# Two-layer PEER decoder trunk: zero columns of the activations written by ScalarE instead of VectorE, small transfers for 16 gathered tokens begun by GpSimd, an index conversion placed later, and one pacing constant 2.0 → 1.85

## The chip, the cores and the metric

The kernel runs on one core of a Trainium2 chip. The metric is the device time of one execution in microseconds (us). Five engines work side by side, each taking its own instructions in order: TensorE (PE, matmul; its weight loads are listed as PEld), VectorE (DVE), ScalarE (ACT), GpSimd (POOL) and SyncE (SP), which here only starts transfers (DMA). An engine's instruction can wait for another engine's or a transfer's semaphore, and what stands behind it on the same engine then waits too.

## The reference, cut

512 tokens of 1024 features pass two layers. Each layer has a mixer (pooling and retention in layer 0, a gated linear recurrence in layer 1) and then PEER, a product-key expert layer, which is where the change lies:

```python
def block(xt):                                   # tokens x 1024
    q = (xt @ w_q).reshape(T, 8, 2, 128)
    s = jnp.einsum('thpd,hpkd->thpk', q, sub_keys)
    s_top, i_top = lax.top_k(s, 16)
    cand = s_top[:, :, 0, :, None] + s_top[:, :, 1, None, :]     # 16 x 16 sums
    cand_id = i_top[:, :, 0, :, None] * 128 + i_top[:, :, 1, None, :]
    best, pos = lax.top_k(cand.reshape(T, 8, 256), 16)
    eid = take_along_axis(cand_id, pos)          # of 16384 experts, 16 per head
    gate = softmax(best)
    act = gelu(einsum('td,thkd->thk', xt, u_tab[eid]))
    return einsum('thk,thkd->td', gate * act, v_tab[eid])
```

Then `h = layer_norm(alpha * h + peer(h))`.

## The kernel before, in words

**Two ways for two kinds of tokens.** For 368 of the 512 tokens (`TN` = 368) PEER is computed densely: all 16384 experts stand in 128 blocks of 128, and each block costs 24 matmuls against `peer_ut` (first product, `mm1`, lines L699 to L708), a gelu on ACT into a tile `ge`, a multiplication by the gate (zero for experts that a token didn't choose, DVE, L1014), and matmuls against `peer_v` (second product, L1049). f32 products are made of three products of a high and a low part: ACT makes the high part `hi` (L132) and DVE the low part `lo` (L133) of every streamed block. The last 144 tokens are not computed densely: POOL gathers their experts' rows (L926). Of these, 16 tokens (`TX`) have columns of their own in the dense accumulators, which is why `ge` has `TD` = 384 columns: the last 16 of each block are zeroed by a DVE memset (L713 in `lookahead`, L991 in `experts`; one memset for a group of `NB` = 4 blocks).

**Stages of one layer's PEER** (`peer`, L654). (1) `route_topk`: queries, top-k and softmax, nearly all on DVE; at its end the ids and gates of a tile of tokens are transposed on PE (L797) and copied into `kT` (ACT L799 to L802, DVE L803). The gates of the first 128 tokens (`gz`) are scattered by POOL with 128 small indirect transfers per layer (L90). (2) `route_gates`, for the other 240 dense tokens: for each group of 8 tokens DVE builds one-hot tiles `oh` (L856) and weighted ones `og` (L857) and PE multiplies them (L866, L867). Two groups are a pair: 32 small matmuls, 15 pairs per layer. ACT copies the result into `gbuf` (L868), and `gd<-gbuf` (2 MB, L875) writes it to memory. (3) `experts`, L954: gates are loaded (`gt<-gd` by SP, L993; `gt<-gz`, L101, the first two by POOL, later ones by SP), multiplied into `ge`, split into `ch` (ACT) and `cl` (DVE), and used by the second product, with the row gathers of POOL and their DVE work (L937, L951) beside.

**What sets the order.** While stages 1 and 2 run, the first products of 56 of the 128 blocks are made ahead of time (`lookahead`, L710) to keep PE busy. A counter (L685 to L691) adds up a cost that the routing yields and takes one block for each 2.8; in the gate stage each pair yields `2 * Y2`. Blocks not taken by the end of stage 2 follow it. `ge` has three buffers; finished groups are written to memory (`sp<-ge`, 768 KB, L719), so a group's first write to `ge` waits until the transfer of the group three before it has landed. The order of the instructions on each engine is fixed when the program is built.

**The 16 gathered tokens' table** `xg` (ids and gates) is filled from `eg` by eight transfers of 2 KB on SP's queue (L873), one per pair; DVE converts the ids to integers (`eidx`, L1001).

Of the kernel before, what the change touches and what calls it, by code (L numbers as in the profile page):

```python
# [20 lines left out]
P = 128  # L21
# [8 lines left out]
NB = 4  # L30
NG = NE // NB
TD = 3 * P
TX = 16
TN = TD - TX
GX = P // TX
GQ = 8
NSD = TD // 32
NLA = 14
# [2 lines left out]
ROT = 3  # L41
RAW = 5
QS = 8
Y2 = 2.0
YC = (0.0, 0.0, 1.0, 4.0)
AHEAD = 4
TAIL = 4
# [58 lines left out]
class Kern:  # L106
# [589 lines left out]
                tb, hs[tb], g1, b1, None if layer else xT, out if layer else None))  # L696
        return xT

    def mm1(self, layer, blk, xT, dst, alt=False):  # L699
        nc = self.nc  # L700
        uh, ul = self.stream(self.io["peer_ut"][layer, blk])
        if alt:
            ps = self.psC.tile([P, 512], F32, name="pC", tag="pC")
        else:
            ps = self.psA.tile([P, 512], F32, name="pA", tag="pA")
        self.mm3(ps[:, :TN], [((uh[:, dc * P:(dc + 1) * P], ul[:, dc * P:(dc + 1) * P]),
                               (xT[0][:, dc, :TN], xT[1][:, dc, :TN])) for dc in range(NDC)])
        nc.scalar.activation(dst[:, :TN], ps[:, :TN], AF.Gelu)  # L708

    def lookahead(self, layer, xT, sp):  # L710
        for g in range(NLA):
            ge = self.pe.tile([P, NB, TD], F32, name="ge", tag="ge", bufs=3)
            self.nc.vector.memset(ge[:, :, TN:], 0.0)  # L713
            for b in range(NB):
                self.mm1(layer, g * NB + b, xT, ge[:, b, :], b % 2 == 1)
                if g >= NLA - KEEP:
                    self.kept[g] = ge
                elif b == NB - 1:
                    self.nc.sync.dma_start(out=sp[g], in_=ge)  # L719
                yield  # L720

    def route_topk(self, layer, xT, kT, gz):
        nc, tc, io = self.nc, self.tc, self.io
        with tc.tile_pool(name="rt", bufs=1) as rt, tc.tile_pool(name="rt2", bufs=2) as rt2, \
# [14 lines left out]
            def choose(tb, h0, n):  # L739
# [47 lines left out]
                n = P - TX if tb == 2 else P  # L787
                if tb == 2:
                    eg = self.eg
                    nc.vector.tensor_copy(eg[:, :, 0], ef.rearrange("p (h s) -> p h s", h=8))  # L790
                    nc.scalar.copy(eg[:, :, 1], gate)
                tg = slice((tb - 1) * P // GW, ((tb - 1) * P + n) // GW)
                ghT, glT = kT[:, tg, 2, :], kT[:, tg, 3, :]
                yield 2.8
# [40 lines left out]
    def route_gates(self, layer, kT, iot, gd):  # L835
        nc, tc = self.nc, self.tc
        W, L = GW, 2
        Q = W // L
        with tc.tile_pool(name="rg", bufs=2) as rg:
            b5 = [P, 2, Q, P, L]  # L840
            for s in range(NSD - NSZ):
                gbuf = rg.tile([P, P, 32], F32, name="gbuf", tag="gbuf")
                if s * 32 + 32 > TN - P:
                    nc.vector.memset(gbuf[:, :, 32 - TX:], 0.0)
                for q in range(32 // W):
                    t0 = s * 32 + q * W
                    if t0 >= TN - P:
                        continue

                    def per(i):  # L850
                        v = kT[:, t0 // W, i:i + 2, :].rearrange("p i (q l) -> p i q l", l=L)
                        return v[:, :, :, None, :].broadcast_to(b5)

                    oh = rg.tile([P, 2, Q, P, L], F16, name="oh", tag="oh")
                    og = rg.tile([P, 2, Q, P, L], F16, name="og", tag="og")
                    nc.vector.tensor_tensor(oh, iot[:, None, None].broadcast_to(b5), per(0), ALU.is_equal)  # L856
                    nc.vector.tensor_tensor(og, oh[:, 1:2].broadcast_to(b5), per(2), ALU.mult)  # L857
                    for r in range(W // 4):
                        if q % 2 and r == W // 4 - 1:
                            pg = self.psC.tile([P, 512], F32, name="pC", tag="pC")  # L860
                        else:
                            pg = self.psB.tile([P, 512], F32, name="pB", tag="pB")
                        for i in range(4):
                            a, b = divmod(r * 4 + i, L)
                            sl = slice(i * P, (i + 1) * P)
                            nc.tensor.matmul(pg[:, sl], oh[:, 0, a, :, b], og[:, 0, a, :, b], start=True, stop=False)  # L866
                            nc.tensor.matmul(pg[:, sl], oh[:, 0, a, :, b], og[:, 1, a, :, b], start=False, stop=True)  # L867
                        nc.scalar.mul(gbuf[:, :, q * W + r * 4:q * W + r * 4 + 4],  # L868
                                      pg.rearrange("p (t k) -> p k t", t=4), 1.0 / GS)
                    if q % 2:  # L870
                        h = t0 // (2 * W)
                        if h < GX:
                            nc.sync.dma_start(out=self.xg[h * TX:(h + 1) * TX], in_=self.eg[P - TX:, h])  # L873
                        yield 2 * Y2
                nc.sync.dma_start(out=gd[:, :, s].rearrange("g p b t -> p g b t"),  # L875
                                  in_=gbuf.rearrange("p (g b) t -> p g b t", b=NB))
# [77 lines left out]
    def experts(self, layer, xT, hs, gd, gz, sp, norm):  # L954
        nc, tc, io = self.nc, self.tc, self.io
        with tc.tile_pool(name="ex", bufs=2) as ex, tc.tile_pool(name="ga", bufs=2) as ga:
# [10 lines left out]
            ges = {}  # L967
# [11 lines left out]
            def front(i):  # L979
                if i >= NE:  # L980
                    return
                g, b = order[i // NB], i % NB
                if b == 0:
                    if g in kept:
                        ge = self.kept[g]
                    else:
                        ge = self.pe.tile([P, NB, TD], F32, name="ge", tag="ge", bufs=3)
                    if g < NLA and g not in kept:
                        nc.sync.dma_start(out=ge, in_=sp[g])
                    elif g >= NLA:  # L990
                        nc.vector.memset(ge[:, :, TN:], 0.0)  # L991
                    gt = ex.tile([P, NSD, NB, 32], F32, name="gt", tag="gt")
                    nc.sync.dma_start(out=gt[:, NSZ:], in_=gd[g])  # L993
                    gz.read(nc.gpsimd if i < 2 * NB else nc.sync, gt[:, :NSZ], g)
                    ges[g] = (ge, gt)
                if g >= NLA:
                    self.mm1(layer, g * NB + b, xT, ges[g][0][:, b, :])

            for i in range(AHEAD):
                front(i)  # L1000
            nc.vector.tensor_copy(self.eidx, self.xg[:, 0])  # L1001
            cs, vs = [], []
            for i in range(NE):
                if i % 2 == 0:
# [2 lines left out]
                if 2 * NB <= i < 2 * NB + GX:  # L1007
                    h = i - 2 * NB
                    nc.sync.dma_start(out=xx[h * TX:(h + 1) * TX], in_=hs[2][P - TX:])
                g, b = order[i // NB], i % NB  # L1010
# [10 lines left out]
                if i < NE - TAIL and i % 2:  # L1021
                    for k in (i - 1, i):
                        for tb in range(3):
                            self.mm2(accs[tb], tb, cs[k], vs[k], k == 0, False)
                used += 1.0 if g < NLA else 2.0
                while done < (P + TX + GQ) * used / (total * 1.02):
                    done += 1
# [155 lines left out]
```

## Time and profile before

| what | value |
|---|---|
| median of 3 runs | 2825.73 us (2825.2 to 2831.99) |
| profiled execution | 2827.84 us, of it span 2826.0 us (first to last instruction) |
| mean granted PE clock | 0.995 of full |
| busy: PE, DVE, ACT, POOL | 99%, 84%, 40%, 45% |

The span is what the trace shows; 1.84 us of the profiled execution lie outside it. The two layers' gate stages run from about 418 to 524 us and from about 1878 to 1983 us of the span, the expert stages from about 553 to 1340 us and from about 2011 to 2780 us. "Granted clock" is the share of full speed (2.4 GHz) at which PE was allowed to run; 0.5 is its lower level, 1.2 GHz.

### The profile page before, as it was taken

To read this page: it belongs to the slowest core of one execution; us is meant where nothing else is said; L and a number is where in the kernel's file an instruction comes from. 1 tells how busy PE (TensorE), PEld (TensorE's weight loads), DVE (VectorE), ACT (ScalarE), POOL (GpSimd) and SP (SyncE) were. 2 spreads that over 40 slices of the span, in tenths; PEclk is the share of its full clock that TensorE was granted. 3 is DMA by queue.
4 is the path that set the end of the run, shared out by engine and by line. 5 is a ranking of instruction groups with operands and counts; after the bars stand their busy time and mean duration, and the time that the engine had idled before them with its cause. 6 is when DMAs were issued, how large, how long until landed. Compare 5 with 4: busy or idle time off the path is not lost. (4 is left out here: it accounts for less than half of the span.)

```text
span 2826.0 us, 42314 instructions
## 1 busy us (share of the span) xinstructions
PE 2786.0 (99%) x15258; PEld 2493.2 (88%) x15258; DVE 2380.9 (84%) x4802; ACT 1120.5 (40%) x1661; POOL 1276.3 (45%) x865
## 2 busy tenths in 40 slices
PE   9999989999999999999999999989999999999998
PEld 7898989988888888888788898989888988888887
DVE  6679988689888889887798689988689898889897
ACT  3334555433333333333334344555333333333332
POOL 0008777245555545543000037885345454445451
PEclk9999999999999999999999999999999999999999
DMA  6355579999999999998322545579999999999994
GB/s 227 124 187 113 138 187 264 295 354 406 356 372 365 370 380 362 355 376 287 101 82 72 204 125 120 150 198 272 339 373 377 364 373 362 379 354 374 351 372 157
DMA packets 316755, 778.32 MB, mean 275 GB/s; under 512 B 62592, under 2 KB 128896, under 8 KB 316544
## 3 DMA queue, kind: packets, MB, share of 16 engines
q1 hardware_dynamic: 196416, 472.40, 47.1%
q0 software_dynamic: 120128, 303.22, 31.0%
q8 instruction: 119, 1.95, 0.3%
q14 instruction: 92, 0.75, 0.1%
HBM read 702.99 MB, written 71.43 MB: 274 GB/s over the span
## 5 line engine op out<-in xcount | busy, mean ns | idle before, releaser
L133 DVE TENSOR_TENSOR lo<-raw,hi 128x1024 fp32r<-128x1024 f32 (+1 forms) x609 | 737.0, 1215 | 176.2 <-ACT hi L132 149.6
L132 ACT CAST hi<-raw 128x1024 fp32r<-128x1024 f32 (+1 forms) x609 | 637.8, 1052 | 595.2 <-PE pA L149 383.1
L148 PE MATMUL pA<-xThi,hi 128*128 128x368 f32 (+2 forms) x2032 | 693.2, 341 | 8.8 <-ACT ge L708 8.8
L149 PE MATMUL pA<-xTlo,hi 128*128 128x368 f32 (+2 forms) x2032 | 690.2, 340 | 0.6 <-DVE xTlo L133 0.6
L150 PE MATMUL pA<-xThi,lo 128*128 128x368 f32 (+2 forms) x2032 | 690.1, 340 | 0.0
L926 POOL DMA_INDIRECT row<-in_u,eid x256 | 396.5, 1549 | 521.8 <-DVE av L937 495.1
L90 POOL DMA_INDIRECT gz<-gate,idx x256 | 462.9, 1808 | 288.2 <-DVE stop L826 170.8
L148 PEld LDWEIGHTS pA<-xThi,hi 128*128 128x128 f32 x2032 | 383.5, 189 | 26.7 <-ACT ge L708 9.4
L149 PEld LDWEIGHTS pA<-xTlo,hi 128*128 128x128 f32 x2032 | 383.6, 189 | 18.2 <-DVE xTlo L133 1.4
L150 PEld LDWEIGHTS pA<-xThi,lo 128*128 128x128 f32 x2032 | 383.4, 189 | 14.5
L926 POOL DMA_INDIRECT row<-in_v,eid x256 | 318.7, 1245 | 165.2 <-DVE h L951 98.8
L132 ACT CAST ch<-ge 128x384 fp32r<-128x384 f32 x256 | 131.5, 514 | 629.8 <-PE pC L1049 538.5
L951 DVE SCALAR_TENSOR_TENSOR h<-row,cf,h 128x1024 f32<-128x1024 f32 x256 | 328.8, 1284 | 5.0 <-DMA row<-in_v,eid 4.8
L937 DVE CUSTOM_DVE_ANT_0 row<-row,x 128x1024 f32<-128x1024 f32 x256 | 311.1, 1216 | 0.4 <-DMA row<-in_u,eid 0.4
L1049 PE MATMUL pC<-hi,ch 128*128 128x512 f32 x768 | 299.9, 390 | 0.0
L1049 PE MATMUL pB<-hi,ch 128*128 128x512 f32 x768 | 299.8, 390 | 0.0
L1049 PE MATMUL pB<-lo,ch 128*128 128x512 f32 x768 | 299.4, 390 | 0.0
L1049 PE MATMUL pB<-hi,cl 128*128 128x512 f32 x768 | 299.3, 390 | 0.0
L1049 PE MATMUL pC<-hi,cl 128*128 128x512 f32 x768 | 299.0, 389 | 0.0
L1049 PE MATMUL pC<-lo,ch 128*128 128x512 f32 x768 | 298.8, 389 | 0.0
L133 DVE TENSOR_TENSOR cl<-ge,ch 128x384 fp32r<-128x384 f32 x256 | 141.6, 553 | 94.8 <-ACT ch L132 93.0
L1014 DVE TENSOR_TENSOR ge<-ge,gt 128x384 f32<-128x384 f32 x256 | 135.5, 545 | 58.1 <-DMA gt<-gz 54.1
(289 smaller groups left out, 4260.5 us busy)
## 6 DMA issues: line engine op xcount, KB each, us to landing
raw<-in_peer_ut SPq DMA_DIRECT2D x256, 512.0 KB
raw<-in_peer_v SPq DMA_DIRECT2D x256, 512.0 KB
gd<-gbuf SPq DMA_DIRECT2D x16, 2048.0 KB
gt<-gd SPq DMA_DIRECT2D x64, 512.0 KB
sp<-ge SPq DMA_DIRECT2D x24, 768.0 KB
ge<-sp SPq DMA_DIRECT2D x24, 768.0 KB
raw<-in_peer_w_q SPq DMA_DIRECT2D x32, 512.0 KB
gz<-zero SPq DMA_DIRECT2D x64, 256.0 KB
```

What stands on the lines that cost most here:

```text
L90: d = nc.gpsimd.indirect_dma_start(out=flat, out_offset=bass.IndirectOffsetOnAxis(ap=idx[:, j:j + 1], axis=0), in_=gate[:, j:j + 1], in_of ...
L132: self.nc.scalar.copy(hi, src)
L133: return self.nc.vector.tensor_tensor(lo, src, hi.bitcast(F32), ALU.subtract)
L148: nc.tensor.matmul(ps, ah, bh, start=(first and i == 0), stop=False)
L149: nc.tensor.matmul(ps, ah, bl, start=False, stop=False)
L150: nc.tensor.matmul(ps, al, bh, start=False, stop=(last and i == n - 1))
L926: nc.gpsimd.indirect_dma_start(out=t, out_offset=None, in_=io[name], in_offset=bass.IndirectOffsetOnAxis(ap=at, axis=0))
L937: nc.vector.tensor_tensor_reduce(ur, ur, x, 1.0, 0.0, ALU.mult, ALU.add, av[:, k:k + 1])
L951: nc.vector.scalar_tensor_tensor(acc, vr, c, acc, ALU.mult, ALU.add)
L1014: nc.vector.tensor_tensor(gv, gv, gt[:, :, b, :], ALU.mult)
L1049: nc.tensor.matmul(acc[hf], a[:, ts], b[:, hf * 512:(hf + 1) * 512], start=first and i == 0, stop=last and i == 2)
```

## The change

Four edits. (a) The 28 + 36 memsets of `ge`'s last columns on DVE go; in their place ACT copies 64 zero columns of the constant tile `sel` (128 x 4x16 elements), right after the gelu of a group's first block. (b) The eight `xg` transfers per layer go from SP's queue to POOL's, issued where `eg` is complete, which on POOL is behind the 128 scatters of `gz`. (c) The conversion to `eidx` comes at the fifth block of the expert stage, tied behind that block's `cl`. (d) `Y2` is 1.85 instead of 2.0, so a pair of gate groups draws 3.7 / 2.8 = 1.32 blocks in place of 4.0 / 2.8 = 1.43.

```diff
-Y2 = 2.0
+Y2 = 1.85
@@ mm1
-    def mm1(self, layer, blk, xT, dst, alt=False):
+    def mm1(self, layer, blk, xT, dst, ge, alt=False):
...
         nc.scalar.activation(dst[:, :TN], ps[:, :TN], AF.Gelu)
+        if ge is not None:
+            nc.scalar.copy(ge[:, :, TN:], self.sel[:, :NB * TX].rearrange("p (b t) -> p b t", b=NB))
@@ lookahead
-            self.nc.vector.memset(ge[:, :, TN:], 0.0)
             for b in range(NB):
-                self.mm1(layer, g * NB + b, xT, ge[:, b, :], b % 2 == 1)
+                self.mm1(layer, g * NB + b, xT, ge[:, b, :], None if b else ge, b % 2 == 1)
@@ route_topk, choose, where tb == 2
                     nc.scalar.copy(eg[:, :, 1], gate)
+                    for h in range(GX):
+                        nc.gpsimd.dma_start(out=self.xg[h * TX:(h + 1) * TX], in_=eg[n:, h])
@@ route_gates
                     if q % 2:
-                        h = t0 // (2 * W)
-                        if h < GX:
-                            nc.sync.dma_start(out=self.xg[h * TX:(h + 1) * TX], in_=self.eg[P - TX:, h])
                         yield 2 * Y2
@@ experts, front
-                    elif g >= NLA:
-                        nc.vector.memset(ge[:, :, TN:], 0.0)
...
-                    self.mm1(layer, g * NB + b, xT, ges[g][0][:, b, :])
+                    self.mm1(layer, g * NB + b, xT, ges[g][0][:, b, :], None if b else ges[g][0])
@@ experts
-            nc.vector.tensor_copy(self.eidx, self.xg[:, 0])
...
+                if i == NB:
+                    with tc.issue_after(mark.ins):
+                        nc.vector.tensor_copy(self.eidx, self.xg[:, 0])
```

Three places of the fixed order, all of layer 0, with the numbers of tiles that tell buffers apart (the same tile can have another number after the change, and L numbers after the change are up to 5 higher).

**First gates, DVE.** Before, from the last `lo` of the blocks ahead to the second group of one-hots:

```order
L133 TENSOR_TENSOR lo_4790<-raw_4787,hi_4789 128x1024 [waits DMAHW6_49,PE_49,Activation_49]
L803 TENSOR_TENSOR kT_1454<-gs_4415,kT_1454 128x14x8 [waits Activation_49]
L713 MEMSET ge_4952 128x4x16 [waits DMAHW0_49]
L856 TENSOR_TENSOR oh_4426<-iot_1455,kT_1454 128x2048 [waits DVE_49,PE_49]
L856 TENSOR_TENSOR oh_4450<-iot_1455,kT_1454 128x2048
L857 TENSOR_TENSOR og_4427<-oh_4426,kT_1454 128x2048 [waits DVE_49]
L857 TENSOR_TENSOR og_4451<-oh_4450,kT_1454 128x2048 [waits DVE_49]
L133 TENSOR_TENSOR lo_4873<-raw_4870,hi_4872 128x1024 [waits DMAHW7_49,PE_49,Activation_49]
```

After, the same stretch:

```order
L133 TENSOR_TENSOR lo_4844<-raw_4841,hi_4843 128x1024 [waits DMAHW6_49,PE_49,Activation_49]
L806 TENSOR_TENSOR kT_1454<-gs_4423,kT_1454 128x14x8 [waits Activation_49]
L859 TENSOR_TENSOR oh_4434<-iot_1455,kT_1454 128x2048 [waits DVE_49,PE_49]
L859 TENSOR_TENSOR oh_4458<-iot_1455,kT_1454 128x2048
L860 TENSOR_TENSOR og_4435<-oh_4434,kT_1454 128x2048 [waits DVE_49]
L860 TENSOR_TENSOR og_4459<-oh_4458,kT_1454 128x2048 [waits DVE_49]
L133 TENSOR_TENSOR lo_4876<-raw_4873,hi_4875 128x1024 [waits DMAHW7_49,PE_49,Activation_49]
```

The memset, which waits for a transfer, stood between `kT` and the first `oh`; it is gone, and nothing stands in its place.

**First gates, ACT, after the change.** `hi` and `ge` are of the blocks ahead, L802 to L805 make `kT`, L871 is the copy of the first gates:

```order
L132 CAST hi_4843<-raw_4841 128x1024 [waits DMAHW6_49,DVE_49,PE_49]
L708 ACTIVATE ge_4384<-pA_4391 128x368 [waits PE_49]
L802 CAST kT_1454<-pC_4418 128x2x14x8 [waits PE_49]
L804 ACTIVATE gs_4423<-pC_4418 128x112
L710 COPY ge_4677<-sel_1034 128x4x16 [waits DMAHW4_49]
L805 CAST kT_1454<-gs_4423 128x14x8 [waits Activation_49]
L132 CAST hi_4875<-raw_4873 128x1024 [waits DMAHW7_49,DVE_49,PE_49]
L708 ACTIVATE ge_4384<-pA_4568 128x368 [waits PE_49]
L871 ACTIVATE gbuf_4433<-pB_4438 128x128x4 [waits DVE_49,PE_49,Pool_49]
```

The copy of zeros for `ge_4677` stands between the two halves of the `kT` work and waits for `sp<-ge_3993`. The one that waits for the same transfer as the memset above (`sp<-ge_4214`) comes some twenty instructions later, behind the gelu of its block. On SP, `sp<-ge_4214` now stands directly behind block loads; before, six of the `xg` transfers stood ahead of it.

**End of the gate stage, DVE.** Before, from the last `og` to the first split of a gated block (`ge_5462` is a group kept in place, `ge_5941` a new one):

```order
L857 TENSOR_TENSOR og_5800<-oh_5799,kT_1454 128x2048 [waits DVE_49]
L133 TENSOR_TENSOR lo_6013<-raw_6010,hi_6012 128x1024 [waits DMAHW4_49,PE_49,Activation_49]
L133 TENSOR_TENSOR lo_6045<-raw_6042,hi_6044 128x1024 [waits DMAHW5_49,PE_49,Activation_49]
L133 TENSOR_TENSOR lo_6086<-raw_6083,hi_6085 128x1024 [waits DMAHW7_49,PE_49,Activation_49]
L133 TENSOR_TENSOR lo_6104<-raw_6101,hi_6103 128x1024 [waits DMAHW0_49,PE_49,Activation_49]
L1014 TENSOR_TENSOR ge_5462<-ge_5462,gt_6075 128x384 [waits DMAHW2_49,DMAHW3_49,DMAHW1_49,DMAHW7_49,DMASW2_49,DVE_49]
L1014 TENSOR_TENSOR ge_5462<-ge_5462,gt_6075 128x384
L1014 TENSOR_TENSOR ge_5941<-ge_5941,gt_5943 128x384 [waits DMAHW6_49,DMASW0_49,Activation_49]
L133 TENSOR_TENSOR lo_6154<-raw_6151,hi_6153 128x1024 [waits DMAHW1_49,PE_49]
L133 TENSOR_TENSOR cl_6080<-ge_5941,ch_6079 128x384 [waits Activation_49]
```

After:

```order
L133 TENSOR_TENSOR lo_6045<-raw_6042,hi_6044 128x1024 [waits DMAHW6_49,PE_49,Activation_49]
L133 TENSOR_TENSOR lo_6085<-raw_6082,hi_6084 128x1024 [waits DMAHW0_49,PE_49,Activation_49]
L1011 TENSOR_TENSOR ge_5510<-ge_5510,gt_6074 128x384 [waits DMASW5_49,DMASW4_49,DMASW6_49,DMASW3_49,DMASW7_49,DMASW2_49,DMAHW3_49,DMASW1_49,DMAHW7_49,DMASW0_49,DVE_49]
L133 TENSOR_TENSOR lo_6103<-raw_6100,hi_6102 128x1024 [waits DMAHW1_49,PE_49,Activation_49]
L1011 TENSOR_TENSOR ge_5510<-ge_5510,gt_6074 128x384 x3
L133 TENSOR_TENSOR lo_6153<-raw_6150,hi_6152 128x1024 [waits DMAHW2_49,PE_49,Activation_49]
L1011 TENSOR_TENSOR ge_5941<-ge_5941,gt_5942 128x384 [waits DMAHW6_49,DMASW0_49,Activation_49]
L133 TENSOR_TENSOR cl_6079<-ge_5941,ch_6078 128x384 [waits Activation_49]
```

Between the first multiplication that waits for gates and the first `cl` there stood two more multiplications and one `lo` before; now there are four more multiplications and two `lo`. On PE the gate stage holds 17.6 blocks of the first product between its first and last gate matmul (18.5 before), and eight whole blocks stand between the last gate matmul and the first second product (seven before).

## Rows read from the trace of the kernel before

**Rows 1.** The page's first part: busy time, share of the span and number of instructions of each engine.

```profile
PE 2786.0 (99%) x15258; PEld 2493.2 (88%) x15258; DVE 2380.9 (84%) x4802; ACT 1120.5 (40%) x1661; POOL 1276.3 (45%) x865
```

**Rows 2.** The waits of PE, by what was waited for: us in total, times, longest us.

```profile
PE pB L866 <- DVE og L857: 13.1, 2, 7.2
PE pA L148 <- ACT ge L708: 8.8, 2, 4.7
```

**Rows 3.** Stretches of the span: length, busy us (and instructions) of each engine, granted PE clock, mean busy share of the DMA engines (it can pass 1 a little), GB/s.

```profile
410.00:420.00 10.00, 4.08 (x33) 3.87 (x32) 5.65 (x6) 2.18 (x4) 8.09 (x5) 0.84 0.72 221
430.00:520.00 90.00, 89.96 (x784) 87.40 (x783) 77.01 (x71) 47.84 (x82) 55.45 (x29) 1.00 0.98 273
560.00:1340.00 780.00, 780.00 (x3871) 691.84 (x3870) 676.53 (x900) 289.16 (x406) 392.03 (x279) 1.00 0.95 363
```

**Rows 4.** Timeline of DVE at the first gates of layer 0, and one row of layer 1: start, us, engine, line, operation, tiles, count [idle before <- what ended it].

```profile
407.98 0.27 DVE L803 TENSOR_TENSOR kT<-gs,kT 128x112 f16<-128x112 f32 x1
414.35 0.11 DVE L713 MEMSET ge<- 128x64 f32 x1 [6.11 <-DMA sp<-ge]
414.39 2.36 DVE L856 TENSOR_TENSOR oh<-iot,kT 128x2048 f16<-128x2048 f16 x2
416.67 2.35 DVE L857 TENSOR_TENSOR og<-oh,kT 128x2048 f16<-128x2048 f16 x2
...
1874.52 0.11 DVE L713 MEMSET ge<- 128x64 f32 x1 [7.24 <-DMA sp<-ge]
```

**Rows 5.** Timeline of PE: the first gate matmul of each layer, two neighbours just behind it, two neighbours of a later gate group, and the matmuls at which the clock rises.

```profile
417.94 0.27 PE L866 MATMUL pB<-og,oh 128*128 128x128 f16 x1 [5.92 <-DVE og L857]
...
418.53 0.31 PE L866 MATMUL pB<-og,oh 128*128 128x128 f16 x1
418.64 0.31 PE L867 MATMUL pB<-og,oh 128*128 128x128 f16 x1
...
423.56 0.38 PE L149 MATMUL pC<-xTlo,hi 128*128 128x368 f32 x1
...
522.51 0.22 PE L867 MATMUL pB<-og,oh 128*128 128x128 f16 x1
522.57 0.22 PE L866 MATMUL pB<-og,oh 128*128 128x128 f16 x1
...
1878.10 0.27 PE L866 MATMUL pB<-og,oh 128*128 128x128 f16 x1 [7.16 <-DVE og L857]
...
1881.05 0.27 PE L866 MATMUL pC<-og,oh 128*128 128x128 f16 x1
```

**Rows 6.** Timeline of SP's DMA queue ahead of the first gates (start, us to issue, line, transfer, count).

```profile
403.48 3.75 SPq L873 DMA_DIRECT2D xg<-eg  x6
...
407.95 0.38 SPq L719 DMA_DIRECT2D sp<-ge  x1
...
1868.11 0.38 SPq L719 DMA_DIRECT2D sp<-ge  x1
```

**Rows 7.** Timelines of SP, ACT, POOL, DVE and PE from the last gates to the first gated blocks, layer 0 and then layer 1, in order of time.

```profile
519.84 7.15 SPq L875 DMA_DIRECT2D gd<-gbuf  x2
525.10 0.62 ACT L868 ACTIVATE gbuf<-pC 128x512 f32<-128x512 f32 x1
537.41 0.80 SPq L993 DMA_DIRECT2D gt<-gd  x2
540.16 0.61 POOL L101 DMA_DIRECT2D gt<-gz  x1
549.87 1.50 DVE L1014 TENSOR_TENSOR ge<-ge,gt 128x384 f32<-128x384 f32 x3 [11.11 <-DMA gt<-gz]
551.28 1.22 DVE L133 TENSOR_TENSOR lo<-raw,hi 128x1024 fp32r<-128x1024 f32 x1
552.76 0.47 ACT L708 ACTIVATE ge<-pA 128x368 f32<-128x368 f32 x1
553.28 0.63 PE L148 MATMUL pA<-xThi,hi 128*128 128x368 f32 x1 [4.70 <-ACT ge L708]
556.47 0.47 PE L149 MATMUL pA<-xTlo,hi 128*128 128x368 f32 x1
556.78 0.33 PE L150 MATMUL pA<-xThi,lo 128*128 128x368 f32 x1
556.95 0.33 PE L148 MATMUL pA<-xThi,hi 128*128 128x368 f32 x1
...
2008.06 1.50 DVE L1014 TENSOR_TENSOR ge<-ge,gt 128x384 f32<-128x384 f32 x3 [10.45 <-DMA gt<-gz]
2011.47 0.67 PE L148 MATMUL pA<-xThi,hi 128*128 128x368 f32 x1 [4.06 <-ACT ge L708]
2017.46 0.44 PE L149 MATMUL pA<-xTlo,hi 128*128 128x368 f32 x1
```

**Rows 8.** Waits of POOL and ACT: us in total, times, longest us.

```profile
POOL gt L101 <- DMA raw<-in_peer_v: 38.0, 1, 38.0
ACT ch L132 <- PE pC L1049: 538.5, 220, 3.6
```

**Rows 9.** Single lines of the program: duration in ns (least/median/most), first and last start in us, forms.

```profile
L713 DVE MEMSET ge<- x28: 112/112/112, 124.5 to 1944.4; 128x64 f32 x28
L802 ACT CAST kT<-gs x4: 285/292/300, 379.3 to 1866.5; 128x128 f16<-128x128 f32 x2, 128x112 f16<-128x112 f32 x2
L1001 DVE CAST eidx<-xg x2: 166/167/168, 425.0 to 1884.9; 128x16 int32<-128x16 f32 x2
```

## The prediction, made before the changed kernel was run

> **What bounds the kernel now.** The page's first part [rows 1] says 99%: PE is busy 2786.0 of 2826.0 us. No other engine can be the bound of the whole, and a change can only win in the 40 us in which PE stands still, and in the time after a stand in which PE runs at its lower clock (which counts as busy). So the second view is PE's waits [rows 2]. Two lines hold 21.9 us of them: the first gate matmul waits for `og` (13.1 us, twice, so once a layer), and a first-product matmul waits for a gelu (8.8 us, twice). The expert stages hold nothing: from 560 to 1340 PE is busy 780 of 780 us at clock 1.00 [rows 3].
>
> Stall 1, the first gates. DVE has `kT` ready at 407.98 + 0.27 = 408.25 us. The next instruction in its queue is the memset, which ends an idle of 6.11 us put down to `sp<-ge`; only then come two `oh` and two `og` [rows 4], and PE starts at 417.94 after 5.92 us [rows 5]. `og` needs nothing of the memset: they share a queue. The transfer is late because SP issues it at 407.95, behind six `xg` transfers that take SP 3.75 us [rows 6]; it lands 6.4 us after its issue (memset at 414.35). Layer 1 is alike: the memset waits 7.24 us, PE 7.16 us.
>
> The stand costs more than itself. After it two gate matmuls follow each other by 0.11 us, later ones by 0.06 [rows 5], and first-product matmuls by 0.31 us against 0.17 [rows 7]. The granted clock of 410 to 420 us is 0.84 [rows 3]: the lower level, 1.2 GHz, after an idle. In layer 0 it lasts until 423.56: 32 gate matmuls lose 0.05 us each (1.6) and some 8 of the block 0.14 each (1.1), 2.7 us together. In layer 1 it lasts from 1878.10 to 1881.05: 28 gate matmuls at 0.05, 1.4 us. Stall 1 costs 5.9 + 2.7 = 8.6 and 7.2 + 1.4 = 8.6, together 17.2 us.
>
> Stall 2, from the gates to the experts [rows 7]. The last gates leave ACT at 525.72; `gd<-gbuf` is issued by 527; SP's `gt<-gd` could only go at 537.41, when that had landed; the second `gt<-gz` goes at 540.16; DVE's first multiplication has its gates at 549.87; the gelu follows at 552.76 and PE at 553.28 after 4.70 us. The lower clock lasts to 556.47: 11 matmuls at 0.14, 1.5 us. Layer 1: 4.06 us, lower clock from 2011.47 to 2017.46, 20 matmuls, 2.8 us. Together 6.2 + 6.9 = 13.1 us.
>
> **The change, part by part.**
>
> *No memset on DVE.* In the new order `oh` stands directly behind `kT`. Before, the first `og` begins 2.3 us after the first `oh` (416.67 − 414.39) and PE starts 1.3 us after that (417.94) [rows 4, 5]; with `oh` at 408.25 that makes PE's start 411.85 us at the earliest. `kT` itself can be later by the copy of zeros that now stands ahead of its last ACT part. No such copy is in the trace; the nearest rows are the cast of 112 columns, 0.29 us, above it [rows 9], and the memset of the same 64 columns on DVE, 0.11 us, below. I take 0.2, nearer the upper: 412.05. PE ran out of work at 417.94 − 5.92 = 412.0 us; the new order gives it one or two matmuls less ahead, some 411.7. So the stand shrinks from 5.9 to 0 to 0.5 us, and with so short a stand I expect no lower clock. Gain: 8.6 − 0.5 = 8.1 us a layer, **16.2 us**.
>
> The cover of this: the memset's wait has gone to ACT, and if the copy of the same buffer came to its turn before `sp<-ge` had landed, ACT would stand. That copy stands some twenty instructions further on in ACT's order, behind three gate pairs and three blocks (about 3 × 5.9 us of PE's time), and SP issues the transfer with no `xg` transfer ahead, so at about 404 instead of 408: landed at about 411, wanted after 425. Hidden; without that cover it would cost up to the 6 us of today.
>
> *64 copies on ACT* of 0.2 to 0.3 us are 13 to 19 us on an engine that is busy 40% of the time [rows 1], and in the expert stages ACT mostly waits for PE to give a buffer back: 538.5 us over 220 waits [rows 8], 2.4 us each. 0 on the path. *64 memsets less* are 7 us less on DVE (0.112 each [rows 9]; the expert stages have the same instruction); where PE never waits, 0.
>
> *Eight `xg` transfers a layer on POOL.* They stand behind the last scatter and ahead of `gt<-gz`. POOL waits 38.0 us there for a transfer's buffer [rows 8]. A plain transfer takes it 0.61 us [rows 7], eight take 4.9: hidden in the 38, and a price only if POOL were later than 537 anyway. On SP they cost as much (3.75 for six). 0 for the move itself. The Trainium skill speaks against it (DMA: Bandwidth & Descriptors, "SWDGE vs HWDGE vs iDMA": a plain transfer belongs on SP or ACT, since GpSimd's descriptors are written by software) and says ("Issuing engines are not separate DMA queues") that another issuer saves only the time of issuing. By its fit of 2.0 us for a small GpSimd transfer, eight in a row would be an estimated 16 us, still inside the 38; the sum is the same by either.
>
> *`eidx` later*: 0.17 us of DVE [rows 9] in another place, 0; the gathers that need it come half-way through the stage.
>
> *`Y2` 1.85.* The same 32 gate groups, one block fewer among them: 24 matmuls of 0.168 are 4.03 us. It doesn't remove work, it moves a block behind the last gates, where PE stands. New timing of stall 2, from the last gate pair's start G (522.32 in layer 0). PE now has the pair (1.84 us) and 7 blocks before the block that needs the late gelu: G + 1.84 + 28.2 = G + 30.05. The chain: gates landed at 537.41 − 522.32 = 15.1, less some 0.7 since the stage is less crowded at its end, 14.4 (the 0.7 is a choice; 0 would cost 0.7 a layer); two gate loads until DVE starts, 549.87 − 537.41 = 12.5; then five multiplications and two `lo` in place of three multiplications, 1.5 + 2 × 0.5 + 2 × 1.1 (each 1.22, a tenth of it beside its neighbour [rows 7]) = 4.7; then 1.9 to the gelu's end. G + 33.5. So the stand is 3.4 us instead of 4.7, and 2.7 instead of 4.1 in layer 1; the lower clock behind it stays. Gain 1.3 + 1.4 = **2.7 us**. Its bounds: −13.1 if both stands and their slow matmuls go, and +6 if the gates land 4 us later because the transfers can't be compressed as PE can (the DMA share is 0.98 from 430 to 520 [rows 3]).
>
> **Sum.** 16.2 + 2.7 = 18.9 us. The profiled execution took 2827.84 us, 2.1 above the median of 2825.73; 2827.84 − 18.9 = 2808.9 on its scale, 2806.8 on the median's. I say 2807 us, 0.67% faster. A difference of 0.3% (8.5 us) is about what a measurement of this kernel can tell from none.
>
> **Rivals.**
>
> *Given back in stall 2.* If the DMA engines, at 0.98, and not PE, set when the gates land, the last landing stays at 537.4 in absolute time. DVE then starts at 549.9, and PE restarts at 556.5 (549.87 + 4.7 + 1.9) in place of 553.2, with one block (4.03) more done: a gain of about 0.8 us a layer in all, 2824 us. For it speaks the 0.98; against it that SP issues the last `gd<-gbuf` within 1.3 us of the last copy by ACT (527.0 and 525.7 [rows 7]), so its queue isn't behind, and that an earlier start moves the transfers earlier too. 0.08.
>
> *The wait only changes engine.* The copy ahead of `kT` (it waits for the `sp<-ge` before) or the next one stops ACT for the transfer, and `kT` or the first `gbuf` copies are late by the same 6 us: 2823 us. Speaks for it: ACT takes its queue in order, and a transfer needs 6.4 us. Against: the transfer in question is issued about 390, 16 us ahead. 0.04.
>
> *Slower: ACT's copies in the expert stages.* There a copy waits until DVE and ACT have given the buffer back, and the casts `ch` and `hi` of the next blocks stand behind it. Today they have 2.4 us to spare [rows 8]. If the 36 copies each held PE by more than (18.9 + 8.5) / 36 = 0.76 us the kernel would be slower than before by 0.3%; at 1.0 us, 2826 − 19 + 36 = 2843. Against it: DVE's multiplication comes before the split on ACT in any case. 0.05.
>
> *Both stalls gone.* If the gates land 3 us earlier than I put them (fewer loads in a stage with one block less), PE never stands, and no clock falls: 2826 − 16.2 − 13.1 = 2797. 0.15.
>
> *Part of it.* Stall 2 grows by 2 to 4 us a layer with its slow matmuls: 2813 to 2817. 0.08. The forecast itself, 2801 to 2813, has 0.60.
>
> **Numbers.** Faster by over 0.3% (under 2817.2): 0.60 + 0.15 + 0.08 = 0.83. Within: 0.08 + 0.04 = 0.12. Slower: 0.05. The range from 2795 to 2820 leaves out the first three rivals, 0.17.
>
> **What would show it.** In the new trace: no wait of DVE for `sp<-ge`; the first `oh` of each layer within 0.3 us of `kT`; PE's wait for `og` there under 1 us (the line of 13.1 falls below 2), and gate matmuls 0.06 us apart from the first on. The copies on ACT at 0.2 to 0.3 us, none with an idle over 1 us ahead of it in the gate stage. PE's wait for the gelu at 5 to 7 us in all instead of 8.8, and first-product matmuls still at 0.31 for a while behind it. The eight `xg` on POOL between the last scatter and `gt<-gz`, the latter still ended by a transfer. Wrong I would be through a late `kT`, a late `gd<-gbuf`, or ACT idle ahead of a copy.

## The result and the profile after

The changed kernel takes 2809.1 us (median of 4 runs, 2806.4 to 2811.1) against 2826.0 of the kernel before on the same chips: ratio 0.9935, 95% interval 0.9918 to 0.9952. The forecast was 2807. The profiled execution took 2806.40 us (span 2804.6), 21.4 less than the one of before; the medians are 16.9 apart. The profiled execution after is the fastest of its four, that of before lay 2 us above its median, so what is added up from the profiles below is 4.5 us more than the medians gained.

The waits of PE in the changed kernel (us in total, times, longest us), the answer to [rows 2]:

```profile
PE pA L148 <- ACT ge L708: 7.2, 2, 4.3
PE pB L869 <- DVE og L860: 0.4, 1, 0.4
```

Stall 1 is gone: 0.4 us instead of 13.1. The timeline of ACT, DVE and PE at the first gates of layer 0 (compare [rows 4, 5]):

```profile
406.47 0.26 ACT L710 COPY ge<-sel 128x64 f32<-128x64 f32 x1
406.99 0.27 DVE L806 TENSOR_TENSOR kT<-gs,kT 128x112 f16<-128x112 f32 x1
407.36 2.36 DVE L859 TENSOR_TENSOR oh<-iot,kT 128x2048 f16<-128x2048 f16 x2
409.64 2.36 DVE L860 TENSOR_TENSOR og<-oh,kT 128x2048 f16<-128x2048 f16 x2
410.91 0.22 PE L869 MATMUL pB<-og,oh 128*128 128x128 f16 x1
410.97 0.22 PE L870 MATMUL pB<-og,oh 128*128 128x128 f16 x1
```

`oh` begins 0.10 us behind `kT`'s end, PE has no idle ahead of its first gate matmul, and gate matmuls are 0.06 us apart from the first on: the clock did not fall.

Stall 2 is still there. SP, POOL, DVE and PE in layer 0, then PE in layer 1 (compare [rows 7]):

```profile
524.58 0.80 SPq L991 DMA_DIRECT2D gt<-gd  x2
525.29 0.57 POOL L101 DMA_DIRECT2D gt<-gz  x1 [4.89 <-DMA raw<-in_peer_v]
536.71 0.56 DVE L1011 TENSOR_TENSOR ge<-ge,gt 128x384 f32<-128x384 f32 x1 [11.52 <-DMA row<-in_u,eid]
541.99 0.56 DVE L133 TENSOR_TENSOR cl<-ge,ch 128x384 fp32r<-128x384 f32 x1 [0.58 <-ACT ch L132]
543.33 0.68 PE L148 MATMUL pA<-xThi,hi 128*128 128x368 f32 x1 [4.33 <-ACT ge L708]
547.79 0.46 PE L150 MATMUL pA<-xThi,lo 128*128 128x368 f32 x1
...
1992.87 0.43 PE L148 MATMUL pA<-xThi,hi 128*128 128x368 f32 x1 [2.87 <-ACT ge L708]
1993.14 0.32 PE L149 MATMUL pA<-xTlo,hi 128*128 128x368 f32 x1
```

In layer 0 PE stands 4.33 us and then runs 15 matmuls at the lower clock (until 547.79); in layer 1 it stands 2.87 us, and this time the clock stays up (0.32 us matmuls behind it).

From the places of PE's first gate matmul, last gate pair and first second product: 417.94, 522.32, 558.95 before and 410.91, 508.94, 549.59 after, so layer 0 gains 7.0 us up to the gates, 6.4 in the gate stage (4.0 of it the block moved, 2.4 the clock) and loses 4.0 behind it (the block moved, and nothing gained on the stand): 9.4. Layer 1 (1878.10, 1981.25, 2018.41 before; 1861.91, 1959.94, 1996.96 after) gains 6.8, 5.1 (4.0 the block, 1.1 the clock) and 0.1, with one block more behind the last gates for nothing: 12.0. Sum 21.4.

### The profile page after: what moved, and what is told of

It is laid out like the page before. It is cut to its first block, busy times and chain, and to the rows that moved or that the text cites. A ratio compares the mean times of both kernels' runs of the same rounds, so it can differ in the third digit from the quotient of the medians.

```text
span 2804.6 us, 42288 instructions
## 1 busy us (share of the span) xinstructions
PE 2777.9 (99%) x15258; PEld 2485.8 (89%) x15258; DVE 2375.4 (85%) x4738; ACT 1127.1 (40%) x1725; POOL 1317.6 (47%) x881
## 4 chain that ended last, share of the span: by engine, by line
PE 89%; DVE 8%; DMA 1%; issue 1%; ACT 0%; POOL 0%; DVEq 0%; SPq 0%; ACTq 0%
PE pB L1049 18%; PE pC L1049 18%; PE pA L148 14%; PE pA L150 14%; PE pA L149 14%; DVE lo L133 2%; PE pC L150 2%; PE pC L148 2%; PE pC L149 2%; PE pB L869 1%; PE pB L870 1%; DVE s L828 1%; DVE ix L830 1%; DMA gt<-gz 1%; PE pB L817 0%
## 5 line engine op out<-in xcount | busy, mean ns | idle before, releaser
L926 POOL DMA_INDIRECT row<-in_u,eid x256 | 402.4, 1572 | 532.8 <-DVE av L937 506.1
L90 POOL DMA_INDIRECT gz<-gate,idx x256 | 486.2, 1899 | 292.9 <-DVE stop L829 168.5
L148 PEld LDWEIGHTS pA<-xThi,hi 128*128 128x128 f32 x2032 | 382.5, 188 | 25.5 <-ACT ge L708 7.8
```

Of the source, the lines that this page charges most:

```text
L90: d = nc.gpsimd.indirect_dma_start(out=flat, out_offset=bass.IndirectOffsetOnAxis(ap=idx[:, j:j + 1], axis=0), in_=gate[:, j:j + 1], in_of ...
L148: nc.tensor.matmul(ps, ah, bh, start=(first and i == 0), stop=False)
L926: nc.gpsimd.indirect_dma_start(out=t, out_offset=None, in_=io[name], in_offset=bass.IndirectOffsetOnAxis(ap=at, axis=0))
```

## Experiments

The theories: **A**, the memset's place in DVE's queue made stall 1; **B**, the `xg` transfers ahead of `sp<-ge` on SP made it; **C**, all that counts is what stands between `kT` and `oh`, by whatever edit it came about; **D**, **E** and **F** on what is left of stall 2.

**Memsets back on DVE, the other three edits kept.**

```diff
-        if ge is not None:
-            nc.scalar.copy(ge[:, :, TN:], self.sel[:, :NB * TX]...)
+            self.nc.vector.memset(ge[:, :, TN:], 0.0)      # in lookahead, and in front for g >= NLA
```

> The changed kernel with the zeros of ge written by memsets on DVE again (the edit a undone, b to d kept). In its order the memset again stands between kT and the first oh and waits for sp<-ge. Theory A (the memset's place in DVE's queue makes the stall): the transfer is now issued at about 404 us, lands about 6 us later at 410 to 411, kT is there at 407.3, so DVE waits about 3 us in each layer, PE's wait for og is 2 to 4 us a layer; 2813 to 2819 us (2813 if the clock doesn't fall after it, 2819 if it does). Theory B (it was the xg transfers ahead of sp<-ge on SP, and without them the memset is harmless): no wait of DVE for sp<-ge, 2809 us as the changed kernel.

2823.5 us (ratio to before 0.9986, 0.9977 to 0.9995). The waits of DVE for `sp<-ge` (us in total, times, longest), then DVE and PE at the first gates of layer 0 and PE in layer 1:

```profile
DVE ge L713 <- DMA sp<-ge: 14.4, 4, 4.7
...
411.35 0.11 DVE L713 MEMSET ge<- 128x64 f32 x1 [3.97 <-DMA sp<-ge]
411.39 2.36 DVE L858 TENSOR_TENSOR oh<-iot,kT 128x2048 f16<-128x2048 f16 x2
414.94 0.27 PE L868 MATMUL pB<-og,oh 128*128 128x128 f16 x1 [3.96 <-DVE og L859]
...
1878.13 0.26 PE L868 MATMUL pB<-og,oh 128*128 128x128 f16 x1 [4.67 <-DVE og L859]
```

Theory A holds and B falls: without any `xg` ahead of it SP issues the transfer at 404.14, it still takes 7.2 us, and the memset still holds DVE. The time is 5 us above what A gave. There are four such waits, not two: of the 14.4 us, 4.0 and 4.7 are these; the other two (4.1 and 1.7) come later in the gate stages, and PE waits 3.7 and 1.2 us for `og` behind them. Beside (b), (c) and (d), edit (a) is worth 14.4 us by the medians.

**`xg` back on SP, the other three kept.**

```diff
-                    for h in range(GX):
-                        nc.gpsimd.dma_start(out=self.xg[...], in_=eg[n:, h])      # route_topk
+                        if h < GX:
+                            nc.sync.dma_start(out=self.xg[...], in_=self.eg[P - TX:, h])   # route_gates
```

> The changed kernel with the eight xg transfers on SP again (edit b undone, a, c, d kept). In its order five xg transfers again stand ahead of the late sp<-ge. Theory A: nothing on PE's path waits for that transfer, since the copy that needs it stands some twenty instructions further on ACT: 2809 us, within 3 us of the changed kernel. Theory B: the late transfer now stops ACT ahead of a copy, kT or gbuf is late, PE's wait for og or gbuf is over 3 us a layer: 2815 us or more.

2810.2 us (0.9938, 0.9924 to 0.9951), the same as the changed kernel. SP's queue:

```profile
403.68 3.12 SPq L874 DMA_DIRECT2D xg<-eg  x5
406.90 0.53 SPq L720 DMA_DIRECT2D sp<-ge  x1
```

SP issues `sp<-ge` behind five `xg`, and neither DVE nor a copy on ACT waits for it. Edit (b) is worth nothing beside the others, as A said.

**Y2 = 1.85 alone, in the kernel before.**

> The kernel before with Y2 = 1.85 alone (edit d alone). The order of the instructions moves too: the memset that waits for the late sp<-ge now stands behind the second pair's og, about 11 us behind kT. Theory C (all that matters is whether a waiting memset stands between kT and the first oh, by whatever edit): no wait there, stall 1 is gone as in the changed kernel, 2807 to 2812 us. Theory A in its narrow form (the gain of stall 1 needs the zeros off DVE): stall 1 stays, only stall 2 moves: 2821 to 2826 us.

2810.5 us (0.9939, 0.9926 to 0.9953): one constant gives what the four edits give, though not in the same places (PE waits 4.7 us for the gelu at stall 2 in the profile, 7.2 in the changed kernel). DVE at the first gates of layer 0, and a later memset:

```profile
408.72 0.27 DVE L803 TENSOR_TENSOR kT<-gs,kT 128x112 f16<-128x112 f32 x1
409.09 2.36 DVE L856 TENSOR_TENSOR oh<-iot,kT 128x2048 f16<-128x2048 f16 x2
...
419.36 0.11 DVE L713 MEMSET ge<- 128x64 f32 x1
...
476.97 0.11 DVE L713 MEMSET ge<- 128x64 f32 x1 [3.08 <-DMA sp<-ge]
```

Theory C. With another pace the blocks fall elsewhere, and the memset that waited stands behind the second pair's `og`, 10 us after SP issued its transfer (409.32), and doesn't wait. A later one waits 3.08 us, though, and PE 2.7 us for `og`; here the memsets still cost something.

**Y2 = 2.0 again, the other three edits kept.**

> The changed kernel with Y2 = 2.0 (edit d undone, a to c kept). Theory A: stall 1 stays gone, 16 to 18 us; stall 2 is as before the change, 4.7 and 4.1 us with the lower clock behind: 2809 to 2812 us. If the constant and not the memset made the gain (theory C in its narrow form): near 2826 us.

2813.5 us (0.9952, 0.9938 to 0.9965), 1.5 above what A gave. No wait of DVE for `sp<-ge`, `oh` at 407.51 right behind `kT` (407.14); but PE waits longer for the gelu at stall 2, with a granted clock of 0.70 and 0.73 in the 10 us around the two stands:

```profile
PE pA L148 <- ACT ge L708: 10.8, 2, 5.9
```

So stall 1 is ended by (d) alone, or by (a) beside (b) and (c); (a) alone was not run. And (d) doesn't end it in every company: beside (b) and (c), without (a), the memset is back between `kT` and `oh` (the first run above). It is the place that counts, not the constant. (d) adds some 4 us here; the intervals of the two ratios overlap, though no run of the one kernel reaches those of the other (2813.1 us and up against 2811.1 and down).

**`eidx` early, the other three kept.**

```diff
+            nc.vector.tensor_copy(self.eidx, self.xg[:, 0])        # ahead of the loop over blocks
-                if i == NB:
-                    with tc.issue_after(mark.ins):
-                        nc.vector.tensor_copy(self.eidx, self.xg[:, 0])
```

> The changed kernel with the conversion to eidx where it stood before in the program (edit c undone, a, b, d kept). In its order the conversion now stands three instructions ahead of kT on DVE and waits for all eight xg transfers, which POOL issues behind its last scatter, at about 514 to 520 us in layer 0. The prediction put edit c at nothing; that holds only where it comes together with edit b. Expected: DVE stands from about 405 to 525 us and likewise in layer 1, PE runs dry after the blocks whose low part is made, so 90 to 115 us longer in each layer: 2990 to 3040 us.

2981.3 us in one run, below the range given: the last scatter was done at 488 us and not at 514, so the `xg` had landed by 493.5. DVE:

```profile
405.70 1.21 DVE L133 TENSOR_TENSOR lo<-raw,hi 128x1024 fp32r<-128x1024 f32 x1
493.48 0.18 DVE L999 CAST eidx<-xg 128x16 int32<-128x16 f32 x1 [86.57 <-DMA xg<-eg]
494.76 0.27 DVE L806 TENSOR_TENSOR kT<-gs,kT 128x112 f16<-128x112 f32 x1
```

A 0.18 us instruction ahead of `kT` costs 86 us a layer (172 in all over the changed kernel; PE waits 172.9 for `og`). So edit (c), at 0 in the sum, is what makes edit (b) possible.

**Row gathers behind the first gate loads** (in the changed kernel).

```diff
+            for p in self.first:             # the two gt<-gz that POOL issues; cut: where they are collected
+                tc.add_manual_dep(d, p.name, LANDED, reason="the first gates come before the rows")
+            self.first = []
```

> The changed kernel with the first row gather of each layer's expert stage made to wait until the first two gate loads have landed, so that POOL issues both gate loads before any row. Theory D (what is left of stall 2 is made by six gathered rows that POOL starts between and behind the two gate loads, so that the second load takes 9.2 us): the second load is issued about 1 us earlier and lands 4 to 6 us after its issue, DVE begins about 531 instead of 536.7 us in layer 0, PE's wait for the gelu falls from 7.2 us to under 2 in all and no clock falls: 2798 to 2803 us. Theory E (the load is slow because block loads, gate writes and the loads of SP fill the transfer engines anyway): it lands near 536 still, 2807 to 2811 us.

2803.7 us (0.9916, 0.9902 to 0.9929), about 5 less than the changed kernel (the intervals of the two ratios overlap), and not quite for the reason given. Stretches of 532 to 538 us (PE clock, DMA share and GB/s last), then POOL's issue and DVE:

```profile
532.00:534.00 2.00, 2.00 (x14) 2.00 (x13) 0.00 (x0) 1.07 (x2) 0.00 (x0) 1.00 0.96 356
534.00:536.00 2.00, 2.00 (x14) 2.00 (x13) 0.00 (x0) 0.35 (x1) 0.00 (x0) 1.00 0.26 90
536.00:538.00 2.00, 2.00 (x14) 2.00 (x13) 1.48 (x2) 0.00 (x0) 0.83 (x1) 1.00 0.00 0
...
527.38 1.11 POOL L101 DMA_DIRECT2D gt<-gz  x2 [4.96 <-DMA raw<-in_peer_v]
536.52 0.56 DVE L1018 TENSOR_TENSOR ge<-ge,gt 128x384 f32<-128x384 f32 x1 [9.28 <-DMA gt<-gz]
```

With no rows the transfer engines drain by 536, yet DVE has its gates only 9.1 us after POOL issued the loads. Theory D is half right: PE's waits are 2.1 and 2.2 us instead of 4.3 and 2.9, but the clock falls in both layers. From the last pair's start DVE has its gates after 25.5 and 25.6 us (27.8 and 26.3 in the changed kernel), 2.2 and 0.7 us less, not 5. Why the loads still take 9 us, with the engines nearly idle at the end of it, stays open.

**Y2 = 1.7 in the changed kernel.**

> The changed kernel with Y2 = 1.7, so 1.21 blocks for a pair of gate groups and one or two blocks more behind the last gates. If the gates land a fixed time behind the last pair (the prediction's way of reckoning), each block behind it covers 4.0 us more and stall 2 is gone: 2798 to 2803 us. If the transfers can't be compressed (the rival that gives the gain back), the gates land as late as they do now in absolute time and stall 2 grows by as much as the gate stage shrinks: 2807 to 2812 us.

2828.0 us (1.0002, 0.9993 to 1.0011): all of the gain is given back, worse than either theory said. DVE and PE, layer 0:

```profile
534.72 1.50 DVE L1011 TENSOR_TENSOR ge<-ge,gt 128x384 f32<-128x384 f32 x3 [15.92 <-DMA row<-in_u,eid]
537.74 1.22 DVE L133 TENSOR_TENSOR lo<-raw,hi 128x1024 fp32r<-128x1024 f32 x1
545.34 0.56 DVE L1011 TENSOR_TENSOR ge<-ge,gt 128x384 f32<-128x384 f32 x1 [6.38 <-DMA gt<-gz]
550.62 0.56 DVE L133 TENSOR_TENSOR cl<-ge,ch 128x384 fp32r<-128x384 f32 x1 [0.58 <-ACT ch L132]
551.96 0.68 PE L148 MATMUL pA<-xThi,hi 128*128 128x368 f32 x1 [11.34 <-ACT ge L708]
```

The last pair starts 6.3 us earlier (502.67 against 508.94), the gates come 2.0 us earlier (534.72 against 536.71): the transfers could be compressed only in part. Most of it is lost at the gate write: the last `gd<-gbuf` goes out 6.8 us earlier (505.61 against 512.38), the load behind it, `gt<-gd`, 2.3 us earlier (522.32 against 524.58). The block or two more behind the last gates would have covered that (the run with the tie at this constant, below, bears it out). But with this constant the multiplications of the third group, whose gates SP loads only at 537.85, also stand on DVE ahead of the first `cl`, and PE waits 11.3 and 11.0 us. The same sort of fault as stall 1, at another place.

**Y2 = 1.7 with the row gathers behind the gate loads too.**

> Both of the two edits before, the row gathers behind the first gate loads and Y2 = 1.7. If theory D holds, stall 2 is already gone and Y2 has nothing left to give: 2798 to 2803 us. If both help in part: the lower of the two, less 1 to 3 us. If neither: 2807 to 2812 us.

2827.6 us (0.9996), which none of the three cases gave: PE waits 22.5 us for the gelu, as without it (22.3), so the rows have no part in this loss.

**The order behind the gates mended** (in the changed kernel).

```diff
-                nc.vector.tensor_tensor(gv, gv, gt[:, :, b, :], ALU.mult)
+                if i < NB:
+                    nc.vector.tensor_tensor(gv, gv, gt[:, :, b, :], ALU.mult)
+                else:
+                    with tc.issue_after(marks[i - NB]):      # the cl of the block four before
+                        nc.vector.tensor_tensor(gv, gv, gt[:, :, b, :], ALU.mult)
...
+                marks.append(mark.ins)                       # mark: the cl of this block
```

> The changed kernel with one tie more: from the fifth block of an expert stage on, a block's multiplication by its gates stands on DVE behind the cl of the block four before it. In its order the first multiplication behind the gates is now that of the first block, with its cl right behind; before, four multiplications of a kept group and two lo stood ahead of it. Theory F (what is left of stall 2 is 4.1 us of DVE's work in the wrong order behind the gates): DVE begins at 536.7 as now, ACT's gelu ends 2.5 us later, near 539.3 instead of 543.3, PE stands 0 to 1 us in each layer and its clock doesn't fall: 2798 to 2803 us. Theory E (the arrival of the gates or the casts on ACT set the end): 2807 to 2811 us.

2797.1 us (0.9898, 0.9881 to 0.9914), 12 us below the changed kernel. DVE and ACT behind the gates, layer 0, then two stretches (PE clock third from the end):

```profile
533.74 0.55 DVE L1012 TENSOR_TENSOR ge<-ge,gt 128x384 f32<-128x384 f32 x1
534.87 0.56 DVE L133 TENSOR_TENSOR cl<-ge,ch 128x384 fp32r<-128x384 f32 x1 [0.58 <-issue]
...
536.46 0.47 ACT L708 ACTIVATE ge<-pA 128x368 f32<-128x368 f32 x1
...
530.00:540.00 10.00, 10.00 (x62) 10.00 (x61) 3.49 (x5) 3.36 (x5) 5.67 (x6) 1.00 1.01 343
540.00:550.00 10.00, 10.00 (x51) 8.90 (x51) 7.72 (x12) 3.67 (x6) 2.34 (x3) 1.00 1.04 377
```

No wait of PE for a gelu is left, and the clock is 1.00 in every stretch there, in layer 1 too. The first multiplication stands at 533.74, straight behind a `lo`, so the gates of the first block's own group were there by then at the latest, 3.0 us ahead of the place (536.71) at which the changed kernel had those of the kept group, and its `cl` follows 1.1 us later instead of 5.3. Theory F, with one thing that it had not counted: it kept DVE's begin at 536.7, but the first block needs only the gates loaded first, and these 3.0 us came on top of the 4.2 us of order.

**The same with Y2 = 1.7.**

> The same tie with Y2 = 1.7, which alone took 2828 us. Theory F: that loss came from multiplications of the third group, whose gates are loaded later (a wait of 6.4 us), that stood on DVE ahead of the first cl; with the tie they stand behind it, and the block more behind the last gates covers the rest: PE doesn't wait for the gelu, 2796 to 2802 us. If the loss came from the gates landing late, by transfers that can't be compressed: 2820 to 2828 us still.

2798.6 us (0.9904, 0.9887 to 0.9920). What cost 19 us without the tie costs nothing with it, so it was the order.

**The same with the rows behind** (Y2 = 1.85).

> The tie together with the row gathers behind the first gate loads (Y2 = 1.85). If the tie alone ends stall 2, the row gathers have nothing left to give: 2798 to 2803 us, within 2 us of the kernel with the tie alone. If each gives part: 2 to 5 us below the better of the two.

2798.3 us (0.9902, 0.9885 to 0.9918). The rows have nothing left to give.

**The kernel before with Y2 = 1.85 and the tie only.**

> The kernel before with Y2 = 1.85 and the tie of the multiplications, and nothing else: memsets on DVE, xg on SP and eidx where they were. In its order the memset that waits stands behind the second pair's og, and the first block's multiplication and cl come first behind the gates. Theories C and F (all that counts is what stands ahead of the first oh and of the first cl on DVE): 2796 to 2802 us, as the changed kernel with the tie. If the edits a, b and c have a worth of their own: 2803 us or more.

2802.4 us (0.9910, 0.9896 to 0.9923), at the edge of what C and F gave and 4 to 5 us above the changed kernel with the tie. The waits of DVE for `sp<-ge`, then DVE and PE in the gate stage of layer 0:

```profile
DVE ge L713 <- DMA sp<-ge: 5.1, 3, 3.5
...
475.75 0.11 DVE L713 MEMSET ge<- 128x64 f32 x1 [3.46 <-DMA sp<-ge]
480.52 0.29 PE L866 MATMUL pB<-og,oh 128*128 128x128 f16 x1 [3.02 <-DVE og L857]
480.61 0.31 PE L867 MATMUL pB<-og,oh 128*128 128x128 f16 x1
```

This is what the memsets on DVE still cost at this pace: PE waits 4.1 us for `og` in all and runs at the lower clock behind the 3.02 (gate matmuls 0.11 us apart). With the copies on ACT, no copy in the gate stages waits at 1.7, 1.85 or 2.0. So edit (a) takes these later waits away too. That it is worth the whole 4 to 5 us is argued: (b) and (c) differ as well, and the intervals of the two ratios overlap.

## Why the prediction was right, point by point

*No memset between `kT` and `oh`: right.* Forecast 16.2 us; measured 7.0 + 2.4 in layer 0 and 6.8 + 1.1 in layer 1, 17.3, of which about 1 us is that `kT` itself was ready at 407.26 instead of 408.25. That part differs between profiles: the first gate comes at 410.91 in the changed kernel and at 412.9 in the one with the rows behind, whose edit lies in the expert stage. The copy on ACT takes 0.23 to 0.28 us, as bounded, and none stops ACT in the gate stage.

*But the reason was too narrow.* It named edit (a) as the cause and gave `Y2` only stall 2. In the changed kernel (a) is a cause, as the run with the memsets back shows; but the constant alone does the same at stall 1, because it moves the memset in the order. The order rows of the changed kernel can't show that, since both edits are in them; the order of each edit alone can.

*Stall 2, forecast 2.7 us:* measured 0 in layer 0 and about 4.1 in layer 1. PE ran out at G + 30.06 (G = 508.94, the last pair's start), forecast 30.05; DVE's chain took 4.7 us, as forecast; the loads 12.1 from SP's issue (12.5). The mis-sized term is the landing of the gates, put at G + 14.4 by a choice: SP's first load goes at G + 15.6. That is the stand of 4.33 us for 3.4. In layer 1 the stand of 2.87 (2.7 forecast) came without the lower clock, which the sum had kept: 2.8 us won that were not counted. Layer 0 gave 1.3 us less than forecast and layer 1 2.7 more; that these nearly cancel is luck. The clock of layer 1 is of one execution, and stands of this length come out both ways (last section), so the slower runs may have lost these 2.8 us; that is not shown.

*`xg` and `eidx` at 0: right in the sum.* Six `xg` take POOL 3.58 us and two 0.49 each (forecast 4.9 in all); POOL is done with all eight 6.2 us after the first begins (514.18 to 520.40), not the 16 of the prediction's other estimate. The cover was far thinner than reckoned: 4.9 us of POOL's waiting are left instead of 38 − 4.9 = 33, because the scatters end at about 515 us and not at 500, and `gt<-gz` now goes at 525 and not at 538. For `eidx` the 0 holds only together with (b): in its old place it costs 86 us a layer. The Trainium skill's preference for SP (DMA: Bandwidth & Descriptors, "SWDGE vs HWDGE vs iDMA") made no difference to the time, as the run with `xg` on SP shows, though a single `xg` landed 5.4 us after POOL's issue and 2.6 after SP's (medians, at different moments of the stage); its sentence that another issuer saves only the issuing agrees with that run too.

*The rivals.* "Given back in stall 2" did not happen at 1.85; at 1.7 the gates kept 4.3 of the 6.3 us, as this rival said, but it took the order on DVE to make a loss of it. ACT's copies in the expert stages hold nothing: PE is busy 780.00 of 780 us from 560 to 1340, as before. What could have made the change worthless was not among the rivals: a pace at which DVE's order behind the gates is worse, 2828 us at 1.7. (The prediction's "32 gate groups" are 30, in 15 pairs of 32 matmuls; no term rests on it.)

## What to carry to other kernels

A pacing constant in a program whose order is fixed when it is built is not a knob on a rate: each value is another order on every engine, and 1.7, 1.85 and 2.0 can differ by 19 us through which waiting instruction happens to stand ahead of a critical one. Before crediting an edit, look at the order of each edit alone, list what stands ahead of the first critical instruction on its engine and what that waits for, and then fix that order by a tie; with it the constant no longer mattered here between 1.85 and 1.7 (2797 and 2799 us; 2.0 was not run with the tie). And a waiting instruction of 0.1 us ahead of critical work costs its wait, not its length, and often the lower clock behind it.

## What was not expected of the hardware

*The clock after a stand.* It fell after every stand of PE of 3.67 us or more (up to 11.3). Below that it went both ways. It stayed up after 2.87 us (above), after 2.66 and 3.08 us (Y2 = 1.85 alone) and after 3.01 and 3.03 us (`xg` on SP, whose profiled execution has a span of 2801.2 us, 6 to 8 less than its other runs). It fell after 2.36 us (memsets back, layer 1) and 3.02 us (1.85 and the tie only), and in the kernel with the rows behind after 2.16 and 2.08 us, there 0.7 and 1.5 us after PE had restarted. PE's timeline of the last, then the first matmul behind 2.36 us (slow) and behind 3.08 us (fast):

```profile
543.14 0.44 PE L149 MATMUL pA<-xThi,hi 128*128 128x368 f32 x1 [2.08 <-ACT ge L709]
543.42 0.33 PE L150 MATMUL pA<-xTlo,hi 128*128 128x368 f32 x1
...
544.82 0.51 PE L149 MATMUL pA<-xThi,hi 128*128 128x368 f32 x1
547.88 0.44 PE L150 MATMUL pA<-xTlo,hi 128*128 128x368 f32 x1
...
2011.66 0.68 PE L148 MATMUL pA<-xThi,hi 128*128 128x368 f32 x1 [2.36 <-ACT ge L708]
...
546.86 0.43 PE L148 MATMUL pA<-xThi,hi 128*128 128x368 f32 x1 [3.08 <-ACT ge L708]
```

So the length of the stand alone doesn't decide it. A fall cost 1.4 to 2.8 us in the kernel before (the prediction's working), so stands of 2 to 4 us make a kernel's time uncertain by some 2 us each. That this makes the changed kernel's spread of 4.7 us is argued and not shown.

*Scatters took longer beside a busy kernel.* The median of the 256 scatter instructions of POOL is 1.62 us before, 1.74 after, up to 1.86 in the kernel with the tie, and 1.55 in the kernel in which DVE and PE stood for 86 us a layer. Whether DVE's work or the traffic slows them was not separated.
